# First-layer expert weights in 512 x 512 pieces, and highest scheduler priority for the activations' short instructions

## The chip, the cores and the metric

The kernel runs on one core of one Trainium2 chip. The metric is the device time of one execution in microseconds (us), the median of several runs. The core's engines work side by side, each through its own queue in order: TensorE (PE, matrix products), VectorE (DVE), ScalarE (ACT), GpSimd (POOL) and SyncE (SP, which here issues most transfers). Transfers run on 16 DMA engines. PE writes its sums into PSUM, from which DVE and ACT read.

## The reference

One layer of a small model over 1024 tokens of width 1024: a layer norm, an attention and a recurrence side by side, a projection, and then a mixture of 32 experts, four of them for each token. Only the experts matter here. All of it is float32.

```python
def clamped_swiglu(hh):
    x_glu = jnp.minimum(hh[..., ::2], SWIGLU_LIMIT)
    x_lin = jnp.clip(hh[..., 1::2], -SWIGLU_LIMIT, SWIGLU_LIMIT)
    return x_glu * jax.nn.sigmoid(SWIGLU_ALPHA * x_glu) * (x_lin + 1.0)

def expert_block(args):
    idx, e = args
    u = clamped_swiglu(h_pad[idx] @ w1[e] + b1[e])
    return u @ w2[e] + b2[e]
```

An expert's first matrix w1 is 1024 x 2048 (gate and linear columns alternate), its second, w2, 1024 x 1024. Each token's four results are weighted by the router's gates and added.

## The kernel before

**Stages.** The mixers and the router take the first 985 us or so; the 32 experts follow in one unrolled loop (`moe`), up to about 2400 us, and a last layer norm ends the kernel. Experts are ranked by how many tokens they have. The 21 lower ranks get up to 128 token slots ("thin", `first`); the 11 upper ones get 136 to 192 ("wide", `first_wide`). They run in a mixed order: thin, wide, thin, wide, then nine times thin, thin, wide, and a last thin one.

**Products in split form.** A float32 factor is split into a high part and a rest (`split`, lines 204 to 206): ACT casts to the high part (hi), DVE subtracts it from the source (lo). A product is then hi x hi, hi x lo and lo x hi (`mm`, lines 193 to 195).

**Pieces.** The weights come in pieces of 1 MB, 128 partitions by 2048 (`piece`, line 1378): eight for w1, four for w2. SP issues a piece's transfer into one of five tiles `w`; ACT casts it in two halves (tile `wsh`, line 205) and DVE subtracts in two halves (tile `wsl`, line 206), into one of four pairs of split buffers. A split buffer is free again when PE has used the piece for the last time; ACT's cast of a later piece waits for that.

**Thin experts.** The gathered rows are transposed by PE and split (`flip`: transposes at line 1374, then a cast on ACT and a subtraction on DVE), giving `xTh` and `xTl`. For each quarter q of the 2048 columns, PE adds the bias (line 1472) and then the products into one accumulator of 512 columns. Here a piece of w1 has all 1024 rows of 256 columns, so an accumulator takes two pieces, each for one half of its columns, with products of 256 columns: 48 for a quarter. The activation follows in four short instructions: a sigmoid on ACT (1482), a clamp (1484), a product (1485) and a second product into `u` (1486) on DVE. `flip` transposes and splits `u` into `uTh` and `uTl`, one quarter late; the last flip is put off into `second` (`late`). The second layer multiplies `uT` with pieces of w2, in products of 512 columns.

**Wide experts.** The tokens are the moving side: `xw` holds hi and lo side by side, and 128 columns of w1 are loaded as weights. One piece gives two accumulators (gate and linear, g = 0, 1); each takes eight products with hi weights (line 1525, up to 384 columns) and eight with lo weights (line 1527). Then come the activation's short instructions (lines 1529 to 1539).

**What sets the order.** The program is recorded in the order of the source; a scheduler then places each engine's instructions by simulated readiness and by priority, which goes by the order of the source. Each engine runs its queue in that order.

## Time and profile before

| | |
|---|---|
| median of 3 runs | 2464.48 us (2464.11 to 2464.49) |
| profiled execution, its own time | 2466.53 us |
| its span, first to last instruction | 2464.7 us |
| PE busy | 2286.7 us (93%) |
| DVE busy | 1996.8 us (81%) |
| ACT busy | 1409.1 us (57%) |
| moved | 567.80 MB, mean 230 GB/s |

Busy shares are averages over the span. A matmul's start is recorded, its end is modelled, and several are under way at once; so PE's pace is read from the distance between starts, not from the busy share. An instruction of DVE that follows another of its kind starts before the recorded end of the one ahead. A wait is put down to what ended last.

### The profile page before, as it was taken

How to read it: one execution, taken by the hardware profiler on the slowest of the kernel's cores; microseconds unless marked ns; L12 is line 12 of the kernel's file. 1: busy time of each engine (PE TensorE's matmuls, PEld its weight loads, DVE VectorE, ACT ScalarE, POOL GpSimd, SP SyncE). 2: the span in 40 equal slices, each digit the busy share in tenths (PEclk: the TensorE clock that was granted, in tenths of full speed). 3: DMA queues.
4: the chain of work that ended last, by engine and by line, in shares of the span. 5: the costliest groups of instructions: out<-in, count | busy, mean ns of one | idle time of the engine just before them, and what ended most of it. 6: DMA issues, size and time to landing. Idle time of an engine off the chain costs nothing. (4 is left out here: it accounts for less than half of the span.)

```text
span 2464.7 us, 42046 instructions
## 1 busy us (share of the span) xinstructions
PE 2286.7 (93%) x15539; PEld 1940.2 (79%) x15539; DVE 1996.8 (81%) x3878; ACT 1409.1 (57%) x2355; POOL 549.3 (22%) x411
## 2 busy tenths in 40 slices
PE   6999989999998995899999999999999999999992
PEld 3776766676765784888898998989889898888981
DVE  7666447777776776788898989898989898898977
ACT  5333335455545433666676767676667676666764
POOL 1005222222213533121211212111212121111113
PEclk9999989999898995999999999999999999999996
DMA  6378542212123323978898979897979898888973
GB/s 268 119 263 278 187 112 56 59 45 58 34 41 90 115 96 128 342 283 290 297 335 296 338 288 337 281 358 275 363 252 336 297 334 302 292 326 300 333 272 139
DMA packets 167335, 567.80 MB, mean 230 GB/s; under 512 B 64617, under 2 KB 79738, under 8 KB 116821
## 3 DMA queue, kind: packets, MB, share of 16 engines
q1 hardware_dynamic: 155476, 524.63, 58.2%
q0 software_dynamic: 11216, 39.34, 6.5%
q8 instruction: 124, 2.03, 0.3%
q10 hardware_dynamic: 432, 1.09, 0.1%
q14 instruction: 87, 0.70, 0.1%
HBM read 508.22 MB, written 56.79 MB: 229 GB/s over the span
## 5 line engine op out<-in xcount | busy, mean ns | idle before, releaser
L206 DVE TENSOR_TENSOR wsl<-w,wsh 128x1024 fp32r<-128x1024 f32 x786 | 932.9, 1218 | 143.6 <-ACT wsh L205 142.1
L205 ACT CAST wsh<-w 128x1024 fp32r<-128x1024 f32 x786 | 782.8, 1047 | 346.6 <-PE acc L195 91.9
L193 PE MATMUL acc<-wsh,xTh 128*128 128x256 f32 x1344 | 381.9, 285 | 10.0 <-ACT xTh L205 5.1
L1525 PE MATMUL acc<-xw,wsh 128*128 128x368 f32 (+7 forms) x1408 | 381.1, 354 | 8.0 <-DVE t L1530 8.0
L194 PE MATMUL acc<-wsl,xTh 128*128 128x256 f32 x1344 | 382.9, 285 | 0.7 <-DVE wsl L206 0.7
L195 PE MATMUL acc<-wsh,xTl 128*128 128x256 f32 x1344 | 381.7, 285 | 0.3 <-DVE xTl L206 0.3
L1527 PE MATMUL acc<-xw,wsl 128*128 128x184 f32 (+7 forms) x1408 | 337.9, 240 | 0.0
L1525 PEld LDWEIGHTS acc<-xw,wsh 128*128 128x128 f32 x1408 | 268.9, 191 | 10.1 <-issue 5.4
L1527 PEld LDWEIGHTS acc<-xw,wsl 128*128 128x128 f32 x1408 | 273.3, 194 | 0.7
L193 PEld LDWEIGHTS acc<-wsh,xTh 128*128 128x128 f32 x1344 | 258.5, 193 | 13.2 <-ACT xTh L205 7.0
L194 PEld LDWEIGHTS acc<-wsl,xTh 128*128 128x128 f32 x1344 | 259.4, 193 | 4.8 <-DVE wsl L206 1.0
L195 PEld LDWEIGHTS acc<-wsh,xTl 128*128 128x128 f32 x1344 | 259.2, 193 | 1.8 <-DVE xTl L206 0.6
L1459 POOL DMA_INDIRECT y_d<-y,idx x42 | 143.0, 3405 | 420.5 <-DVE y L1451 333.3
L1362 POOL DMA_INDIRECT xg<-h_d,idx x43 | 97.7, 2273 | 615.7 <-issue 272.2
L193 PE MATMUL acc<-wsh,uTh 128*128 128x512 f32 x512 | 203.5, 400 | 19.2 <-ACT uTh L205 19.2
L194 PE MATMUL acc<-wsl,uTh 128*128 128x512 f32 x512 | 202.4, 396 | 0.0
L195 PE MATMUL acc<-wsh,uTl 128*128 128x512 f32 x512 | 193.6, 406 | 1.3 <-DVE uTl L206 1.3
L193 PEld LDWEIGHTS acc<-wsh,uTh 128*128 128x128 f32 x512 | 97.3, 190 | 40.7 <-ACT uTh L205 21.8
L193 PE MATMUL sm<-hTh,wsh 128*128 128x512 f32 x288 | 115.0, 400 | 6.4 <-ACT wsh L205 2.0
L194 PE MATMUL sm<-hTl,wsh 128*128 128x512 f32 x288 | 115.6, 401 | 4.2 <-DVE hTl L347 3.1
L195 PE MATMUL sm<-hTh,wsl 128*128 128x512 f32 x288 | 113.5, 395 | 0.0
L194 PEld LDWEIGHTS acc<-wsl,uTh 128*128 128x128 f32 x512 | 97.8, 191 | 19.3 <-DVE wsl L206 0.2
(584 smaller groups left out, 4323.5 us busy)
## 6 DMA issues: line engine op xcount, KB each, us to landing
w<-in_w_dram SPq DMA_DIRECT2D x384, 1024.0 KB
aw<-in_ada_dram SPq DMA_DIRECT2D x34, 512.0 KB
w<-in_w_in_dram SPq DMA_DIRECT2D x18, 512.0 KB
aw<-in_ada_dram SPq DMA_DIRECT2D x7, 1024.0 KB
rkv_d<-stage SPq DMA_DIRECT2D x12, 512.0 KB
xt<-in_x_dram SPq DMA_DIRECT2D x8, 512.0 KB
xr<-in_x_dram SPq DMA_DIRECT2D x8, 512.0 KB
xr_d<-xr SPq DMA_DIRECT2D x8, 512.0 KB
```

What stands on the lines that cost most here:

```text
L193: mm(out, a.hi, b.hi, start=start, stop=False)
L194: mm(out, a.hi, b.lo, start=False, stop=False)
L195: mm(out, a.lo, b.hi, start=False, stop=stop)
L205: (hi_eng or self.nc.scalar.copy)(dst.hi, src)
L206: (lo_eng or self.nc.vector).tensor_tensor(dst.lo, src, dst.hi.bitcast(F32), ALU.subtract)
L1362: self.nc.gpsimd.indirect_dma_start(out=xg[0:n], out_offset=None, in_=self.h2_d, in_offset=bass.IndirectOffsetOnAxis(ap=idx[0:n, 0:1], axi ...
L1459: nc.gpsimd.indirect_dma_start(out=self.y_d, out_offset=bass.IndirectOffsetOnAxis(ap=idx[0:n, 0:1], axis=0), in_=y[0:n], in_offset=None, c ...
L1525: nc.tensor.matmul(acc[:, 0:2 * cap], w.hi[:, c], xw[:, k].rearrange("p a t -> p (a t)"), start=(k == 0), stop=False)
L1527: nc.tensor.matmul(acc[:, 0:cap], w.lo[:, c], xw[:, k, 0], start=False, stop=(k == KD - 1))
```

## The change

Three edits, all in the experts.

1. The host lays out w1 so that a piece holds 512 rows of 512 columns (four blocks of 128 rows) instead of 1024 rows of 256. Size and number of the pieces stay.
2. A thin expert's quarter still takes two pieces, but each is now one half of the rows for all 512 columns: 24 products of 512 columns instead of 48 of 256. A wide expert takes two pieces at a time, for two column blocks j; each of its four accumulators needs both.
3. The short instructions of the activations, and the flips of `u`, are recorded under the scheduler's highest priority.

```diff
-    w1 = f("exp_w1")[0].reshape(NE, KD, P, 8, P, 2)
-    o["w1"] = w1.transpose(0, 3, 2, 1, 5, 4).reshape(NE, 8, P, KD, 256)
+    w1 = f("exp_w1")[0].reshape(NE, 2, 4, P, 4, 2, P, 2)
+    o["w1"] = w1.transpose(0, 4, 1, 3, 2, 5, 7, 6).reshape(NE, 8, P, 4, 512)
...
-            for j in range(2):
-                ws = self.piece(w1[bass.ds(e, 1), 2 * q + j].rearrange("o p k n -> (o p) (k n)"))
-                for k in range(KD):
-                    w, c = ws[k // 4], k % 4 * 256
-                    self.mm(acc[:, j * 256:(j + 1) * 256], xT[:, k], w[:, c:c + 256],
-                            start=False, stop=(j == 1 and k == KD - 1))
...
+            for m in range(2):
+                ws = self.piece(w1[bass.ds(e, 1), 2 * q + m].rearrange("o p k n -> (o p) (k n)"))
+                for k in range(4):
+                    c = k % 2 * 512
+                    self.mm(acc, xT[:, 4 * m + k], ws[k // 2][:, c:c + 512], start=False, stop=(m == 1 and k == 3))
+            with self.tc.high_priority():
...
+                S.activation(v2(sg), a[:, :, 0], AF.Sigmoid, scale=1.702)
...
+                if q:
+                    self.flip(uT, u, 2 * q - 2, 2 * q)
+
+        def late():
+            with self.tc.high_priority():
+                self.flip(uT, u, 6, 8)
+        return [uT], late
...
-            ws = self.piece(w1[bass.ds(e, 1), j].rearrange("o p k n -> (o p) (k n)"))
+            if j % 2 == 0:
+
+                ws = []
+                for m in range(2):
+                    ws += self.piece(w1[bass.ds(e, 1), j + m].rearrange("o p k n -> (o p) (k n)"))
...
+                a = j % 2 * 2 + g
                 for k in range(KD):
-                    w = ws[k // 4]
-                    c = slice(k % 4 * 256 + g * P, k % 4 * 256 + (g + 1) * P)
+                    w, c = ws[k // 2], slice(k % 2 * 512 + a * P, k % 2 * 512 + (a + 1) * P)
...
+                with self.tc.high_priority():
+                    t = mp.tile([P, cap], F32, name=f"t{g}")
...
```

In the rows of the built programs below, a name's number tells one buffer's use from another; `wsh_` and `wsl_` with neighbouring numbers are one piece. PE in a thin expert, where one piece of a quarter ends and its other one begins. Before:

```order
L193 MATMUL acc_16542<-wsh_16546,xTh_16300 128x256
L194 MATMUL acc_16542<-wsl_16547,xTh_16300 128x256
L195 MATMUL acc_16542<-wsh_16546,xTl_16301 128x256
L193 MATMUL acc_16542<-wsh_16578,xTh_16300 128x256
L194 MATMUL acc_16542<-wsl_16579,xTh_16300 128x256
L195 MATMUL acc_16542<-wsh_16578,xTl_16301 128x256
```

and now:

```order
L193 MATMUL acc_15606<-wsh_15610,xTh_15436 128x512
L194 MATMUL acc_15606<-wsl_15611,xTh_15436 128x512
L195 MATMUL acc_15606<-wsh_15610,xTl_15437 128x512
L193 MATMUL acc_15606<-wsh_15630,xTh_15436 128x512
L194 MATMUL acc_15606<-wsl_15631,xTh_15436 128x512
L195 MATMUL acc_15606<-wsh_15630,xTl_15437 128x512
```

The products are twice as wide and half as many: twelve of them use up a piece, where 24 did.

PE in a wide expert, from the last products of the second accumulator's first four row blocks on. Before:

```order
L1525 MATMUL acc_15872<-xw_15697,wsh_15846 128x336
L1527 MATMUL acc_15872<-xw_15697,wsl_15847 128x168
L1525 MATMUL acc_15852<-xw_15697,wsh_15846 128x336
L1527 MATMUL acc_15852<-xw_15697,wsl_15847 128x168
L1525 MATMUL acc_15852<-xw_15697,wsh_15846 128x336
```

and now (line 1533 is the former 1525, line 1535 the former 1527):

```order
L1533 MATMUL acc_15016<-xw_14833,wsh_14982 128x336
L1535 MATMUL acc_15016<-xw_14833,wsl_14983 128x168
L1533 MATMUL acc_14996<-xw_14833,wsh_14990 128x336
L1535 MATMUL acc_14996<-xw_14833,wsl_14991 128x168
L1533 MATMUL acc_14996<-xw_14833,wsh_14990 128x336
```

The third row is the 17th product of the expert. It stood on the first piece (wsh_15846), and stands now on the second (wsh_14990); before, the second piece came after all 32 products of the first and twelve of the second layer of the expert ahead.

DVE at the start of the same wide expert, from the first accumulators' read on; `wsl` rows are the weights' subtractions, the third and fourth piece here. Before:

```order
L206 TENSOR_TENSOR wsl_15961<-w_15958,wsh_15960 128x1024 x2
L206 TENSOR_TENSOR uTl_15393<-tr_15767,uTh_15392 128x256
L1339 SCALAR_TENSOR_TENSOR idx_15737<-tr_15728,at_15739 128x1
L1354 TENSOR_REDUCE gate_15738<-tr_15728 128x1
L1530 TENSOR_TENSOR t0_15869<-acc_15852,t0_15869 128x168
L206 TENSOR_TENSOR wsl_16018<-w_16015,wsh_16017 128x1024 x2
L1530 TENSOR_TENSOR t1_15889<-acc_15872,t1_15889 128x168
L1451 SCALAR_TENSOR_TENSOR y_15832<-acc_15745,gate_14797,g2p_8911 128x512
L1451 SCALAR_TENSOR_TENSOR y_15832<-acc_15746,gate_14797,g2p_8911 128x512
L1535 TENSOR_SCALAR t1_15889<-t1_15889 128x168
```

and now (lines 1539, 1545, 1546 and 1547 are the former 1530, 1535, 1536 and 1537):

```order
L1354 TENSOR_REDUCE gate_14874<-tr_14864 128x1
L1539 TENSOR_TENSOR t0_15013<-acc_14996,t0_15013 128x168
L1539 TENSOR_TENSOR t1_15033<-acc_15016,t1_15033 128x168
L1545 TENSOR_SCALAR t1_15033<-t1_15033 128x168
L1546 SCALAR_TENSOR_TENSOR t1_15033<-t0_15013,t1_15033 128x168
L1547 SCALAR_TENSOR_TENSOR t1_15033<-sg_15036,t1_15033 128x168
L1451 SCALAR_TENSOR_TENSOR y_14968<-acc_14881,gate_14125,g2p_8911 128x512
L1451 SCALAR_TENSOR_TENSOR y_14968<-acc_14882,gate_14125,g2p_8911 128x512
L206 TENSOR_TENSOR uTl_14979<-t1_15033,uTh_14978 128x128
L206 TENSOR_TENSOR u1_8914<-t1_15033,u1_8914 128x40
L206 TENSOR_TENSOR wsl_15105<-w_15102,wsh_15104 128x1024 x2
```

The whole chain of the first column block, nine short instructions, now stands ahead of the fourth piece's subtraction, where one stood before.

## Rows read from the trace of the kernel before

**Rows 1.** The page, busy time: us, share of the span, instructions.
```profile
PE 2286.7 (93%) x15539; PEld 1940.2 (79%) x15539; DVE 1996.8 (81%) x3878; ACT 1409.1 (57%) x2355; POOL 549.3 (22%) x411
```
**Rows 2.** Table by stage: stretch, length, busy us by engine, granted clock, DMA share, GB/s.
```profile
core 0: us, PE busy (x) PEld busy (x) DVE busy (x) ACT busy (x) POOL busy (x), PEclk, DMA share, GB/s
1443.00:1480.00 37.00, 37.00 (x259) 34.06 (x258) 35.47 (x43) 27.21 (x34) 8.80 (x2) 1.00 0.87 322
1480.00:1518.00 38.00, 36.91 (x270) 34.07 (x269) 37.33 (x50) 26.61 (x34) 14.24 (x4) 1.00 0.91 333
1518.00:1575.00 57.00, 57.00 (x385) 52.24 (x384) 48.85 (x104) 37.04 (x74) 5.04 (x4) 1.00 0.82 297
1575.00:1611.00 36.00, 36.00 (x256) 33.28 (x255) 35.51 (x44) 27.05 (x33) 7.52 (x2) 1.00 0.91 323
1611.00:1649.00 38.00, 36.90 (x269) 33.93 (x268) 37.34 (x50) 26.59 (x35) 9.70 (x4) 1.00 0.93 343
```
**Rows 3.** PE in time order, a thin first layer: start us, us, engine, line, operation.
```profile
1596.08 0.28 PE L195 MATMUL acc<-wsh,xTl 128*128 128x256 f32 x1
...
1598.96 0.28 PE L195 MATMUL acc<-wsh,xTl 128*128 128x256 f32 x1
```
**Rows 4.** PE in time order, two second layers of thin experts.
```profile
1179.10 0.39 PE L193 MATMUL acc<-wsh,uTh 128*128 128x512 f32 x1
...
1182.05 0.39 PE L194 MATMUL acc<-wsl,uTh 128*128 128x512 f32 x1
...
1607.61 0.40 PE L193 MATMUL acc<-wsh,uTh 128*128 128x512 f32 x1
...
1608.77 0.39 PE L195 MATMUL acc<-wsh,uTl 128*128 128x512 f32 x1
```
**Rows 5.** The page, costliest groups: count | busy us, mean ns | idle before, releaser.
```profile
L193 PE MATMUL acc<-wsh,xTh 128*128 128x256 f32 x1344 | 381.9, 285 | 10.0 <-ACT xTh L205 5.1
L194 PE MATMUL acc<-wsl,xTh 128*128 128x256 f32 x1344 | 382.9, 285 | 0.7 <-DVE wsl L206 0.7
L195 PE MATMUL acc<-wsh,xTl 128*128 128x256 f32 x1344 | 381.7, 285 | 0.3 <-DVE xTl L206 0.3
```
**Rows 6.** PE in time order, start of the wide expert at 1525.
```profile
1525.31 0.41 PE L1525 MATMUL acc<-xw,wsh 128*128 128x336 f32 x1
...
1527.41 0.35 PE L1525 MATMUL acc<-xw,wsh 128*128 128x336 f32 x1
...
1529.26 0.35 PE L1525 MATMUL acc<-xw,wsh 128*128 128x336 f32 x1
...
1532.55 0.31 PE L1525 MATMUL acc<-xw,wsh 128*128 128x336 f32 x1
```
**Rows 7.** DVE in time order, the same expert's second and fourth piece.
```profile
1523.36 2.35 DVE L206 TENSOR_TENSOR wsl<-w,wsh 128x1024 fp32r<-128x1024 f32 x2
...
1530.99 2.36 DVE L206 TENSOR_TENSOR wsl<-w,wsh 128x1024 fp32r<-128x1024 f32 x2 [0.69 <-ACT wsh L205]
```
**Rows 8.** Waits from 985 to 2405 us: us in total, times, longest.
```profile
ACT sg L1482 <- PE acc L195: 62.6, 51, 8.0
ACT wsh L205 <- DMA w<-in_w_dram: 16.0, 10, 4.5
PE acc L193 <- ACT uTh L205: 11.5, 9, 3.0
```
**Rows 9.** PE in time order near 1778 us, and that stretch by stage.
```profile
1778.35 0.50 PE L193 MATMUL acc<-wsh,uTh 128*128 128x512 f32 x1 [2.18 <-ACT uTh L205]
...
1778.94 0.63 PE L193 MATMUL acc<-wsh,uTh 128*128 128x512 f32 x1
1779.36 0.63 PE L194 MATMUL acc<-wsl,uTh 128*128 128x512 f32 x1
...
1775.00:1782.00 7.00, 4.82 (x21) 3.69 (x19) 6.36 (x11) 3.74 (x7) 0.00 (x0) 0.78 1.00 422
```

More of the change, by code (lines that the diff above doesn't have):

```diff
@@ L1472, in first @@
             nc.tensor.matmul(acc, self.pick[:, q:q + 1].to_broadcast([P, P]), bs, start=True, stop=False)
-            for j in range(2):
-                ws = self.piece(w1[bass.ds(e, 1), 2 * q + j].rearrange("o p k n -> (o p) (k n)"))
-                for k in range(KD):
-                    w, c = ws[k // 4], k % 4 * 256
-                    self.mm(acc[:, j * 256:(j + 1) * 256], xT[:, k], w[:, c:c + 256],
-                            start=False, stop=(j == 1 and k == KD - 1))
-            a = acc.rearrange("p (j g f) -> p j g f", j=2, g=2)
-            v2 = lambda t: t.rearrange("p (j f) -> p j f", j=2)
-            sg = mp.tile([P, 256], F32, name="sg")
-            S.activation(v2(sg), a[:, :, 0], AF.Sigmoid, scale=1.702)
-            ln = mp.tile([P, 256], F32, name="ln")
-            V.tensor_scalar(v2(ln), a[:, :, 1], 8.0, -6.0, ALU.min, ALU.max)
-            V.scalar_tensor_tensor(v2(ln), a[:, :, 0], 7.0, v2(ln), ALU.min, ALU.mult)
-            V.scalar_tensor_tensor(u[:, q * 256:(q + 1) * 256], sg, SIG7, ln, ALU.min, ALU.mult)
-            if q:
-                self.flip(uT, u, 2 * q - 2, 2 * q)
-        return [uT], lambda: self.flip(uT, u, 6, 8)
+            for m in range(2):
[4 more added lines that the diff above has]
+            with self.tc.high_priority():
+                a = acc.rearrange("p (j g f) -> p j g f", j=2, g=2)
+                v2 = lambda t: t.rearrange("p (j f) -> p j f", j=2)
+                sg = mp.tile([P, 256], F32, name="sg")
+                S.activation(v2(sg), a[:, :, 0], AF.Sigmoid, scale=1.702)
+                ln = mp.tile([P, 256], F32, name="ln")
+                V.tensor_scalar(v2(ln), a[:, :, 1], 8.0, -6.0, ALU.min, ALU.max)
+                V.scalar_tensor_tensor(v2(ln), a[:, :, 0], 7.0, v2(ln), ALU.min, ALU.mult)
+                V.scalar_tensor_tensor(u[:, q * 256:(q + 1) * 256], sg, SIG7, ln, ALU.min, ALU.mult)
+                if q:
[4 more added lines that the diff above has]
+        return [uT], late
     def load_x(self, rows):
@@ L1527, in first_wide @@
                     nc.tensor.matmul(acc[:, 0:cap], w.lo[:, c], xw[:, k, 0], start=False, stop=(k == KD - 1))
-                t = mp.tile([P, cap], F32, name=f"t{g}")
-                S.activation(t, acc[:, cap:2 * cap], AF.Identity, bias=bc[:, 2 * j + g:2 * j + g + 1])
-                V.tensor_tensor(t, acc[:, 0:cap], t, ALU.add)
-                parts.append(t)
-            gl, ln = parts
-            sg = mp.tile([P, 256], F32, name="sg")[:, 0:cap]
-            S.activation(sg, gl, AF.Sigmoid, scale=1.702)
-            V.tensor_scalar(ln, ln, 8.0, -6.0, ALU.min, ALU.max)
-            V.scalar_tensor_tensor(ln, gl, 7.0, ln, ALU.min, ALU.mult)
-            V.scalar_tensor_tensor(ln, sg, SIG7, ln, ALU.min, ALU.mult)
-            self.split(u0[:, j], ln[:, 0:P])
-            self.split(Split(u1[:, j, 0, 0:n1], u1[:, j, 1, 0:n1]), ln[:, P:cap])
+                with self.tc.high_priority():
+                    t = mp.tile([P, cap], F32, name=f"t{g}")
+                    S.activation(t, acc[:, cap:2 * cap], AF.Identity, bias=bc[:, 2 * j + g:2 * j + g + 1])
+                    V.tensor_tensor(t, acc[:, 0:cap], t, ALU.add)
+                    parts.append(t)
+            with self.tc.high_priority():
+                gl, ln = parts
+                sg = mp.tile([P, 256], F32, name="sg")[:, 0:cap]
+                S.activation(sg, gl, AF.Sigmoid, scale=1.702)
+                V.tensor_scalar(ln, ln, 8.0, -6.0, ALU.min, ALU.max)
+                V.scalar_tensor_tensor(ln, gl, 7.0, ln, ALU.min, ALU.mult)
+                V.scalar_tensor_tensor(ln, sg, SIG7, ln, ALU.min, ALU.mult)
+                self.split(u0[:, j], ln[:, 0:P])
+                self.split(Split(u1[:, j, 0, 0:n1], u1[:, j, 1, 0:n1]), ln[:, P:cap])
         return [u0, u1], None
```

## The prediction

> **What bounds the kernel now.** I read the page's busy list first [rows 1]: TensorE (PE) is busy 93% of the span, VectorE (DVE) 81%, ScalarE (ACT) 57%. That is an average over a mixer part and an expert part, so the table by stage comes next [rows 2]. It covers thin, thin, wide, thin, thin expert from 1443 to 1649 us. In every row PE is busy for at least 36.9 of 38 us at a granted clock of 1.00. DVE is busy for 35.5 of 37, 37.3 of 38 and 37.3 of 38 us in the thin rows, but only for 48.9 of 57 in the wide one. The 16 DMA engines are at 0.82 to 0.93. So PE sets the pace of the experts, DVE follows within 1 to 2 us of every thin expert, and only a wide expert gives DVE time to catch up. The reader should keep these two together: whatever PE saves in two thin experts in a row, DVE has to save as well, or draw from its lead.
>
> A busy PE is not a PE at its peak, so I counted how far apart its products start. The 256-column products of a thin first layer stand 24 steps apart in 1598.96 - 1596.08 = 2.88 us: 0.120 us each [rows 3]. The 512-column products of the second layer make 13 steps in 1182.05 - 1179.10 = 2.95 us, 0.227 us each, and in a slower place 5 steps in 1608.77 - 1607.61 = 1.16 us, 0.232 us each [rows 4]. The second layer's weights come in the same type and through the same split, so these rows stand for the new 512-column products.
>
> **Wider products in thin experts.** 21 thin experts hold 1344 products in each of three lines [rows 5], 4032 in all. They become 2016 of twice the width. Before: 4032 x 0.120 = 483.8 us. After: 2016 x 0.2275 = 458.6 us. That is 25.2 us less on PE; by the slower step, 2016 x 0.232 = 467.7, it is 16.1. I take 25.2, since the clean stretches are the common case, and keep 16 as an end. Nothing covers this work now, so it comes off the path as long as PE stays the bound. Bytes, transfers, casts and subtractions keep their number and size: a piece is 128 x 2048 before and after. Transfers cost nothing by my sum: ACT waited for a weight transfer 10 times, 16.0 us in all [rows 8]; if the cover were gone, one piece would cost at most the longest of those, 4.5 us.
>
> A rule of the Trainium skill speaks against this term. The page TensorE: Matmul & The Clock Gate, section Back-to-back issue gap, gives a warm product's step as its columns over 2.4 GHz plus 2.5 ns: 109.2 ns for 256 columns, 215.8 ns for 512. By that rule halving the count saves 2.5 ns a pair, 5.0 us in all, instead of 25.2. The rows differ from it at both widths (120 and 227 ns), and they decide.
>
> **Pairs of pieces in wide experts.** The same matrix is now cut so that a wide expert needs two pieces before it can end any accumulator. The products of a wide expert keep number, width and weight loads: PE's own time is unchanged. What moves is when the second piece is needed. Before, the first product on the second piece starts at 1532.55, 7.24 us after the first product of the expert at 1525.31 [rows 6]. By the order of the changed program it is the 17th product, behind eight pairs. A pair takes (1529.26 - 1527.41) / 7 = 0.264 us [rows 6], so it is needed after 2.1 us: 5.1 us sooner. Its subtraction on DVE ended at 1523.36 + 2.35 = 1525.71 [rows 7], 6.8 us ahead of need. That cover shrinks to 1.7.
>
> Two more things eat it. First, over the two thin experts ahead PE gains 2 x (192 x 0.120 - 96 x 0.2275) = 2.4 us, while DVE's work there, 35.5 + 37.3 = 72.9 of 74 us [rows 2], stays. Its idle 1.1 us absorb part at best, so 1.3 to 2.4 us of lead are lost. Secondly, the wide expert ahead of the pair now gives its split buffers back later: in the order, five fewer 512-column products lie between the release and the first product of the next thin expert, 5 x 0.2275 = 1.1 us of lead, of which some or none may bite. So the cover ends between 1.7 - 1.3 = +0.4 and 1.7 - 2.4 - 1.1 = -1.8. I take a wait of 1.0 us. There are nine places where two thin experts stand ahead of a wide one: 9 us given back, between 0 and 16.
>
> Inside a wide expert the bursts cost nothing by my sum. The order puts nine short DVE instructions, where one stood, ahead of the fourth subtraction. But DVE is idle there for 57 - 48.9 = 8 us [rows 2], and the fourth piece is first needed behind a whole pair of pieces' products. If that cover were gone, each pair would wait about the 0.7 us that DVE waited for ACT in the row shown [rows 7].
>
> **Highest priority for the short instructions.** It changes places in four queues, not work. On ACT a sigmoid that waits for its accumulator holds the casts queued behind it; PE accumulators kept it waiting 51 times for 62.6 us already, and nobody on PE felt that, since ACT is 57% busy. On PE the transposes of the activations (line 1374) and the second layer's first product stand behind the short chain; PE lost 11.5 us in nine waits for the cast of a transposed activation [rows 8]. By the order the last flip of a thin expert stands some 1.5 us nearer to its accumulator, because PE has less to do between, and the chain on DVE has about as many subtractions in it as before. So I expect these waits neither gone (-11.5) nor doubled (+11.5), but a little more: +0.4 us in each of nine pairs, +4 us. POOL and SP keep their order; POOL's waits are on no path here.
>
> **The clock.** One PE wait of 2.18 us for such a cast was followed by products 0.42 us apart, and that stretch of 7 us was granted 0.78 of the clock [rows 9]: part of it ran at 1.2 instead of 2.4 GHz, and PE lost (1 - 0.78) x 7 = 1.5 us. A wait of 1.0 us is well under 2.18; I take 0, and keep 1.5 us for each of nine places as an end.
>
> **The sum.** -25.2 + 9 + 4 = -12.2 us. The profiled execution took 2466.5 us, 1.8 more than its span of 2464.7 and 2.0 more than the median of the runs, 2464.48. The edit lies wholly in the span, so I take the same difference off the median: 2452 us.
>
> **The rivals.**
> - The cover holds, and no wait comes at the wide experts: then the flips balance too, and PE's 25.2 us all arrive: 2439. For it: DVE's lead in a wide expert is 8 us of idle time. Against it: the cover sums to zero only at its best end.
> - DVE becomes the bound of the thin pairs. If the wait is 2.4 us in each of nine places (22 us) with the flips' 4 us, the gain is gone: 2465. For it: DVE's 72.9 of 74 us. Against it: it needs more than the worse end of my cover.
> - Slower: the wait for the second piece reaches the length after which half speed followed. With 3.0 us of wait and 1.5 us of half speed in nine places and the flips' 4 us the price is 44.5 us against 25.2: 2484. It decides from (25.2 - 4) / 9 = 2.4 us for wait and clock together, which the worst cover, 1.8, passes once half speed follows. For it: [rows 9]. Against: 3.0 us are 1.2 more than the worst cover.
> - The wide product is no bargain: if a first-layer product of 512 columns steps at 0.2375 us, just above the slow rows, PE saves only 5.0 us, and with 13 us given back the time is 2472. Against it: [rows 3, 4]. The rule of the Trainium skill named above (TensorE: Matmul & The Clock Gate, Back-to-back issue gap) gives the same saving by other steps.
>
> **How the numbers follow.** Forecast 0.58, cover holds 0.13, DVE the bound 0.14, half speed 0.10, no bargain 0.05. A measurement of this kernel can tell about 0.2%, 5 us, from no change: 2459.5 to 2469.4. The forecast itself spreads from 2444 to 2460, its give-back running from some 5 to 20 us; a small part of it lies within 0.2%. So faster 0.68 (0.55 + 0.13), same 0.17 (0.03 + 0.14), slower 0.15 (0.10 + 0.05). The range runs from 2438, just under the full saving, to 2468, just over the case where DVE binds; it leaves out half speed and the case of no bargain.
>
> **What would show it.** First-layer products of 512 columns starting 0.227 us apart, 96 to a thin expert plus four bias products, say the first term. PE's busy time and the stretch of a thin pair shrinking by less than 2.4 us, with DVE at 73 of some 73 us, say that DVE binds there. A PE wait of about 1 us for DVE's second subtraction at the start of a wide expert, with its first product on the second piece some 2 us after the first, says the second term. PE waiting for the cast of a transposed activation for clearly more or less than 11.5 us judges the third. The granted clock in those starts judges the slow rival. I am wrong in the main if the steps are not 0.227, or if PE waits inside the wide experts, at each pair of pieces, rather than at their start.

## The result, and the profile after

The changed kernel is **slower**, by 0.57%: 2476.52 us (median; 2463.43 for the kernel before, run beside it). The ratio is 1.0057, with a 95% interval of 1.0043 to 1.0070, so about 14 us are lost where the prediction had 12 gained; the time lies above its range. One of its 22 executions took 3185.47 us at a mean granted clock of 0.643, and is not in the ratio. The profiled execution took 2468.29 us, 8 us under its kernel's median, against 2466.53 before, 3 over. Executions of one kernel differ by some 10 us either way, so sums from two profiles hold to about that, and only ratios over many executions decide below which kernel is faster.

First the page of the changed kernel, busy time, and the three lines that answer to [rows 1, 5] (count | busy us, mean ns | idle before):

```profile
PE 2264.4 (92%) x13523; PEld 1824.5 (74%) x13523; DVE 1997.7 (81%) x3878; ACT 1405.3 (57%) x2353; POOL 482.5 (20%) x411
...
L193 PE MATMUL acc<-wsh,xTh 128*128 128x512 f32 x672 | 263.5, 395 | 4.5 <-ACT wsh L205 4.0
L194 PE MATMUL acc<-wsl,xTh 128*128 128x512 f32 x672 | 264.7, 394 | 0.5 <-DVE wsl L206 0.5
L195 PE MATMUL acc<-wsh,xTl 128*128 128x512 f32 x672 | 264.4, 394 | 0.0
```

The products are half as many. Their steps, PE in time order in a thin first layer (start us, us), nine steps between the two rows:

```profile
1596.42 0.39 PE L195 MATMUL acc<-wsh,xTl 128*128 128x512 f32 x1
...
1598.46 0.39 PE L195 MATMUL acc<-wsh,xTl 128*128 128x512 f32 x1
```

(1598.46 - 1596.42) / 9 = 0.227 us, as [rows 4] had it. So PE saved what was forecast. The table by stage, with the columns of [rows 2], for thin, thin, wide, thin, thin of the changed kernel, shows where it went:

```profile
1439.60:1478.70 39.10, 36.16 (x148) 28.07 (x147) 35.89 (x44) 26.53 (x33) 7.31 (x2) 0.92 0.89 339
1478.70:1519.40 40.70, 38.37 (x194) 31.15 (x193) 38.19 (x51) 28.36 (x37) 5.11 (x4) 0.99 0.84 300
1519.40:1575.90 56.50, 56.50 (x377) 51.76 (x377) 47.60 (x100) 35.76 (x71) 3.65 (x3) 1.00 0.79 283
1575.90:1615.10 39.20, 36.11 (x148) 28.17 (x147) 35.93 (x45) 26.63 (x33) 6.55 (x2) 0.92 0.89 336
1615.10:1655.90 40.80, 38.46 (x195) 31.13 (x193) 38.20 (x52) 28.34 (x37) 5.43 (x4) 0.99 0.84 299
```

A thin pair (two thin experts in a row) took 74 us before [rows 2] and takes 39.2 + 40.8 = 80.0 now. The wide expert shown is nearly unchanged. Over the loop it looks otherwise: counted from an expert's first product on PE (the bias product, in a thin one) to the next expert's first one, the nine thin pairs took 680.2 us before and take 702.5 now, and the eleven wide experts took 634.3 and take 620.5. So the pairs lose 22 us and the wide experts win 14; both come back below. In both thin rows PE *and* DVE stand idle for some 2.3 to 3.3 us: neither is the bound any more. What PE waited for, from 985 to 2405 us (us in total, times, longest):

```profile
PE acc L193 <- ACT uTh L205: 20.5, 17, 1.9
PE acc L195 <- DVE uTl L206: 13.5, 11, 1.7
PE tr L1330 <- DVE uTl L206: 10.6, 9, 1.2
...
PE tr L1374 <- DVE uTl L206: 3.7, 10, 0.4
PE acc L1533 <- DVE t L1539: 3.2, 1, 3.2
PE tr L1374 <- DVE u L1486: 1.3, 1, 1.3
```

All but the line of L1533 are waits on the flips of `u` (three of them through the buffers of the transposes and through `u` itself): 49.6 us. Before, the same view had 11.5 us for uTh [rows 8] and these lines:

```profile
PE acc L1525 <- DVE t L1530: 8.0, 8, 2.0
...
PE acc L195 <- DVE uTl L206: 1.3, 2, 1.1
PE tr L1374 <- DVE u L1486: 0.7, 1, 0.7
```

That makes 13.5 us on flips, so there are 36 us of new waits against some 28 us of work saved. The wide experts' wait for DVE's read of an accumulator (L1525, now L1533) fell from 8.0 to 3.2 us.

One place of a flip, at the end of the first layer of the thin expert that starts at 1576 us. PE, DVE and ACT in time order (in brackets, idle time ahead and what ended it):

```profile
1604.59 0.79 PE L1374 MATMUL tr<-csts,u 128*128 128x128 f32 x4
1607.14 0.50 PE L193 MATMUL acc<-wsh,uTh 128*128 128x512 f32 x1 [1.77 <-ACT uTh L205]
...
1610.15 1.22 PE L195 MATMUL acc<-wsh,uTl 128*128 128x512 f32 x2 [0.93 <-DVE uTl L206]
```
```profile
1604.47 0.41 DVE L1486 SCALAR_TENSOR_TENSOR u<-sg,ln 128x256 f32<-128x256 f32 x1
1604.80 3.49 DVE L206 TENSOR_TENSOR wsl<-w,wsh 128x1024 fp32r<-128x1024 f32 x3
1608.21 0.42 DVE L1485 SCALAR_TENSOR_TENSOR ln<-acc,ln 128x256 f32<-128x256 f32 x1
1608.54 1.22 DVE L206 TENSOR_TENSOR wsl<-w,wsh 128x1024 fp32r<-128x1024 f32 x1
1609.67 0.42 DVE L206 TENSOR_TENSOR uTl<-tr,uTh 128x256 fp32r<-128x256 f32 x1
```
```profile
1604.83 1.99 ACT L205 CAST wsh<-w 128x1024 fp32r<-128x1024 f32 x2 [0.71 <-PE acc L195]
1606.73 0.36 ACT L205 CAST uTh<-tr 128x256 fp32r<-128x256 f32 x1
```

The four transposes are done by 1605.4. The cast `uTh` stands behind two casts of weights on ACT, and `uTl` behind four subtractions of weights on DVE. In PE's queue nothing stands between the transposes and the first product on `uTh`, so PE idles twice, 2.7 us in all. The clock follows (table by stage of the two stretches, granted clock third from the end of each row):

```profile
1604.00:1611.00 7.00, 3.91 (x15) 2.37 (x14) 7.00 (x12) 2.92 (x6) 0.00 (x0) 0.86 1.00 404
1611.00:1616.00 5.00, 5.00 (x13) 3.84 (x13) 1.76 (x4) 1.99 (x2) 0.00 (x0) 0.51 0.82 338
```

For 5 us PE was granted 0.51, so it ran nearly all the time at 1.2 instead of 2.4 GHz, which costs (1 - 0.51) x 5 = 2.5 us more. Over all experts, though, the clock is the same in both kernels, by the third number from the end of the two rows (before, then after):

```profile
965.00:2430.00 1465.00, 1406.99 (x9684) 1290.56 (x9684) 1315.09 (x2119) 984.17 (x1509) 272.50 (x103) 0.98 0.84 305
```
```profile
965.00:2430.00 1465.00, 1389.34 (x7651) 1180.67 (x7652) 1309.29 (x2113) 979.47 (x1505) 201.31 (x101) 0.98 0.83 304
```

**A budget of PE.** From the first bias product of the experts to the last product of a second layer I took each step from one start to the next. The median step of its form (line, tiles and shapes) is work; an excess of about one more such step is half speed; an excess above 0.3 us is a wait; what is left is small excess. In us, from one profile each (the other kernels are explained below):

| kernel | length | work | half speed | waits | small |
|---|---|---|---|---|---|
| before | 1460.4 | 1367.4 | 23.1 | 62.2 | 7.7 |
| after | 1468.8 | 1338.9 | 22.9 | 91.1 | 15.9 |
| new pieces, products of 256 | 1463.6 | 1369.4 | 20.8 | 65.4 | 8.0 |
| old pieces, clamp on ACT | 1424.4 | 1366.1 | 14.1 | 37.4 | 6.8 |
| new pieces, clamp on ACT | 1410.6 | 1338.5 | 11.5 | 45.4 | 15.2 |

How finely the forms are told apart moves some 3 us between work, half speed and small excess; the length and the waits stay. Before to after: work -28.5, waits +28.9, small excess +8.2, half speed -0.2.

### The profile page after: what moved, and what is told of

Its sections match the earlier page's. It is cut to its first block, busy times and chain, and to the rows that moved or that the text cites. A ratio compares the mean times of both kernels' runs of the same rounds, so it can differ in the third digit from the quotient of the medians.

```text
span 2466.2 us, 38048 instructions
## 1 busy us (share of the span) xinstructions
PE 2264.4 (92%) x13523; PEld 1824.5 (74%) x13523; DVE 1997.7 (81%) x3878; ACT 1405.3 (57%) x2353; POOL 482.5 (20%) x411
## 3 DMA queue, kind: packets, MB, share of 16 engines
q8 instruction: 108, 1.77, 0.3%
## 4 chain that ended last, share of the span: by engine, by line
PE 33%; DVE 20%; issue 5%; ACT 2%; DMA 1%; SPq 0%; POOLq 0%; POOL 0%; DVEq 0%; ACTq 0%
DVE wsl L206 14%; PE acc L1533 11%; PE acc L195 6%; PE acc L193 5%; PE acc L194 5%; PE acc L1535 4%; ACT wsh L205 1%; DMA w<-in_w_dram 1%; PE tr L1374 1%; PE acc L1439 1%; PE acc L1435 1%; DVE ln L1484 1%; DVE uTl L206 1%; DVE oh L1326 1%; DVE y L1451 1%
## 5 line engine op out<-in xcount | busy, mean ns | idle before, releaser
L1533 PE MATMUL acc<-xw,wsh 128*128 128x368 f32 (+7 forms) x1408 | 373.7, 350 | 3.3 <-DVE t L1539 3.2
L1533 PEld LDWEIGHTS acc<-xw,wsh 128*128 128x128 f32 x1408 | 265.0, 189 | 4.7 <-issue 3.4
L193 PE MATMUL acc<-wsh,xTh 128*128 128x512 f32 x672 | 263.5, 395 | 4.5 <-ACT wsh L205 4.0
L194 PE MATMUL acc<-wsl,xTh 128*128 128x512 f32 x672 | 264.7, 394 | 0.5 <-DVE wsl L206 0.5
L195 PE MATMUL acc<-wsh,xTl 128*128 128x512 f32 x672 | 264.4, 394 | 0.0
L193 PE MATMUL acc<-wsh,uTh 128*128 128x512 f32 x512 | 207.8, 409 | 28.5 <-ACT uTh L205 22.1
L1459 POOL DMA_INDIRECT y_d<-y,idx x42 | 121.6, 2896 | 490.7 <-DVE y L1451 382.2
L195 PE MATMUL acc<-wsh,uTl 128*128 128x512 f32 x512 | 201.4, 418 | 13.6 <-DVE uTl L206 13.5
L1362 POOL DMA_INDIRECT xg<-h_d,idx x43 | 58.9, 1370 | 624.1 <-DVE xTl L206 221.5
L193 PEld LDWEIGHTS acc<-wsh,xTh 128*128 128x128 f32 x672 | 127.7, 190 | 31.3 <-ACT wsh L205 4.2
L194 PEld LDWEIGHTS acc<-wsl,xTh 128*128 128x128 f32 x672 | 127.5, 190 | 28.0 <-DVE wsl L206 1.0
L195 PEld LDWEIGHTS acc<-wsh,xTl 128*128 128x128 f32 x672 | 127.3, 189 | 26.9 <-DVE xTl L206 0.2
L195 PEld LDWEIGHTS acc<-wsh,uTl 128*128 128x128 f32 x512 | 96.8, 197 | 40.3 <-DVE uTl L206 21.6
```

The source lines that it names most:

```text
L193: mm(out, a.hi, b.hi, start=start, stop=False)
L194: mm(out, a.hi, b.lo, start=False, stop=False)
L195: mm(out, a.lo, b.hi, start=False, stop=stop)
L1362: self.nc.gpsimd.indirect_dma_start(out=xg[0:n], out_offset=None, in_=self.h2_d, in_offset=bass.IndirectOffsetOnAxis(ap=idx[0:n, 0:1], axi ...
L1459: nc.gpsimd.indirect_dma_start(out=self.y_d, out_offset=bass.IndirectOffsetOnAxis(ap=idx[0:n, 0:1], axis=0), in_=y[0:n], in_offset=None, c ...
L1533: nc.tensor.matmul(acc[:, 0:2 * cap], w.hi[:, c], xw[:, k].rearrange("p a t -> p (a t)"), start=(k == 0), stop=False)
```

## The experiments

Theories, by the letters that the expectations use. **A**: the raised priority places the flips badly. **B**: the chain from a quarter's accumulator to its flip keeps its length, while PE with wider products reaches the flip's first use sooner. **C**: DVE paces the thin pairs, whatever PE is seen to wait for. **D**: the wide experts' pairs of pieces cost the lead. **E**: the split buffers limit how far ACT and DVE run ahead. **F**: the cut of the pieces itself costs. Each ratio is to the kernel before on the same chip, with its 95% interval.

**The priority.** New pieces without any raised priority (`e1`); old pieces with it (`e2`); new pieces with it in thin (`e3`) or wide experts (`e4`) alone.

```diff
-            with self.tc.high_priority():
+            if True:
```

> The new pieces (512 rows x 512 columns, thin and wide experts) without any raised priority. Theory A (the raised priority places the flips of u badly): the waits of PE on the cast and the subtraction of u's transposes, 48 us in the changed kernel (uTh 20.5, uTl 13.5, transposed slots behind uTl 10.6, transposes behind uTl 3.7) against 13 before, fall back to about 13, and the 25 us saved on PE arrive: 12 to 25 us faster than before, 2440 to 2452. Theory B (the shape alone: PE has less to do between a quarter's end and the first use of its flip, while the casts and subtractions queued ahead of the flip are as many): those waits stay near 48 us and the kernel is within 0.3% of the changed one, 5 to 20 us slower than before. Theory C (DVE paces the thin pairs): the waits go from the flips to the subtractions of weights, and the time stays within 5 us of before.

> The pieces of before (1024 rows x 256 columns) with the raised priority at all the places of the change. Theory A: PE's waits on the flips of u rise from 13 us to 40 us or more, and the kernel is 20 to 40 us slower than before. Theory B: the waits stay within 10 us of before's 13, the time within 0.3% of before. Theory C: as B.

> The new pieces in both kinds of expert, the raised priority only in the thin experts. If A holds through the thin experts' flips, this is as slow as the changed kernel (within 0.2%). If the harm comes from the wide experts' short instructions under raised priority (they run ahead of casts and subtractions of the pieces that the next thin expert needs), it is as fast as the kernel without any priority. Theory B: as the changed kernel within 0.3%.

> The new pieces in both kinds of expert, the raised priority only in the wide experts: the other half of the pair. A through the thin experts' flips: as fast as the kernel without any priority, 12 to 25 us under before. A through the wide experts: as slow as the changed kernel. Theory B: as the changed kernel within 0.3%.

Measured: e1 1.0069 (1.0044 to 1.0093), e2 0.9993 (0.9968 to 1.0018), e3 1.0070 (1.0043 to 1.0097), e4 1.0068 (1.0044 to 1.0092). A falls: the priority is worth nothing, and the pieces are the whole loss. The order of the experts' instructions in the traces says why. With the new pieces, taking the priority away changes the instruction at 2 of 7668 places on PE, 2 of 1511 on ACT and 6 of 2141 on DVE, and each of PE's waits on flips is the same to 0.3 us. So what the front's order rows show of bunched short instructions comes from the pieces, not from the priority.

**Which expert, and which part of the cut.** From here on the new pieces come without raised priority. `e5` has new pieces in thin experts alone, `e6` in wide ones alone (a second copy of the weights in the other layout serves the rest). `e13` has new pieces in both, but two products of 256 columns for one of 512:

```diff
-                    self.mm(acc, xT[:, 4 * m + k], ws[k // 2][:, c:c + 512], start=False, stop=(m == 1 and k == 3))
+                    for h in range(0, 512, 256):
+                        self.mm(acc[:, h:h + 256], xT[:, 4 * m + k], ws[k // 2][:, c + h:c + h + 256],
+                                start=False, stop=(m == 1 and k == 3 and h == 256))
```

> The new pieces in the thin experts alone; a second copy of the weights in the old layout serves the wide experts, whose code is as before; no raised priority. The run with the new pieces and no priority was 0.69% slower than before, so the pieces are the cause; this one tells in which kind of expert. Theory B (in the thin experts PE runs short of work between the end of a quarter and the first use of its flip; DVE and ACT reach the flip no sooner): the full loss is here, 10 to 20 us slower than before. Theory D (the pairs of pieces in the wide experts cost the lead that the thin ones need): the loss is not here, and the 25 us of PE arrive: 12 to 25 us faster than before.

> The new pieces in the wide experts alone; the thin ones have the old layout and the old code, 256 columns to a product; no raised priority. Theory B: within 5 us of before. Theory D: PE gains nothing in the thin experts and the wide ones lose what the whole change lost beside its gain: 20 to 40 us slower than before.

> New pieces in both kinds of expert, no raised priority, but a thin expert's first layer multiplies each 512-column block in two products of 256 columns, as before the change; PE has the 28 us back that the profile shows it lost. Theory B (the products' width: what PE no longer does in products comes back as waits for the flips, and more): within 0.3% of before, 8 to 15 us under the same kernel with 512 columns, with some 30 us fewer waits of PE. Theory F (the cut of the pieces itself costs, whatever the products' width): 15 to 30 us above the kernel with 512 columns, 2490 to 2505.

Measured: e5 1.0125 (1.0096 to 1.0154), e6 1.0018 (0.9995 to 1.0041), e13 1.0019 (0.9999 to 1.0038). The thin experts hold the loss, as B says, and more of it than the whole change (28 us, where B had 10 to 20): the wide experts' pairs of pieces give back about 0.6% where the thin experts have the new pieces, though alone they win nothing. D falls, and so does F: the new cut with the old width is as fast as before, within the interval. It is the **width of the products** that costs, by 0.5%, though it takes work off PE. PE's waits of e13, in the same view as above:

```profile
PE tr L1330 <- DVE uTl L206: 12.7, 9, 1.4
PE acc L193 <- ACT uTh L205: 8.9, 11, 0.9
...
PE acc L195 <- DVE uTl L206: 3.3, 9, 0.5
PE tr L1374 <- DVE uTl L206: 1.1, 2, 0.8
```

26.0 us on flips, where 512 columns give 49.6. But 26.0 is already twice the 13.5 of before. `e6`, whose thin experts are as before, has 27.8 us of these waits, and its instructions stand in the same order as e13's on ACT and DVE and, but for a dozen places, on PE. So some 13 of the 36 us of new waits come with the wide experts' pairs of pieces, and some 23 with the width. The first part costs no time, because the wide experts win as much. Length and PE's waits by kind of expert, counted and told apart as above, in us, from one profile each:

| kernel | nine thin pairs | waits there | eleven wide experts | waits there |
|---|---|---|---|---|
| before | 680.2 | 19.7 | 634.3 | 14.4 |
| e6, new pieces in wide experts alone | 695.1 | 30.5 | 619.0 | 3.7 |
| e13, new pieces, products of 256 | 693.1 | 30.8 | 619.2 | 3.9 |
| after | 702.5 | 56.3 | 620.5 | 3.7 |

The flips show how both parts arise. I read three means from the traces, over the first experts of the nine pairs, for quarters 0, 1 and 2 (us): the chain from the end of a quarter's accumulator to `u`; PE's work, in median steps, between that end and the first product on the quarter's flip; and how long before its first product `uTl` is ready.

| kernel | chain to `u` | PE's work until the first use | `uTl` ready ahead by |
|---|---|---|---|
| before | 8.7, 8.1, 8.1 | 18.2, 15.4, 13.5 | 2.4, 1.8, 2.4 |
| e13 | 11.4, 11.0, 11.2 | 18.2, 15.2, 13.7 | 0.1, 0.1, 0.3 |
| after | 11.9, 10.4, 12.0 | 17.3, 14.2, 13.1 | (PE waits) |

The wide experts' pairs of pieces make the chain there 3 us longer: 8 to 9 subtractions of weights stand in it, where 6 to 7 stood. In e6 the three chains are the same to 0.1 us. That uses up the lead of the flips, and PE just gets by. The wide product then takes 0.6 to 1.0 us of PE's work away over each flip, 2.5 us in a pair and some 22 in nine, and PE's waits in these experts rise from 4.0 us in e13 to 25.5. That is B, on top of a chain that had grown. As a mean over all 72 quarters of the pairs the chain is as long as ever (9.2 us before, 8.7 in e13, 9.0 after), which hides this, because it is shorter in the second experts' first quarter (8.9 before, 4.4 after).

One thing stays open. With the width the scheduler's order changes too: the first flip of such an expert had 5.1 us of PE's work between its transposes and its first use before, 1.9 in e13 and 0.5 with 512 columns. No run holds the order and changes the width alone, so the share of this placing is not known.

**Without the dependence.** In `e7` (new pieces) and `e8` (before) a thin expert's second layer multiplies the split rows of x, while the flips still run.

```diff
-            self.second(e, slots[i], uT, late, i == NE - 1)
+            u2 = [x[i]] if late else uT
+            self.second(e, slots[i], u2, late, i == NE - 1)
```

> New pieces in both kinds of expert, no raised priority; the second layer of a thin expert multiplies the split rows of x in the place of the split activations, so nothing on PE but the transposes themselves depends on a flip of u. The flips are still carried out, and DVE, ACT and PE have the same number of instructions. It leaves out the use of the activations, and its output isn't the reference's. Theory B (latency of the flips): PE's waits for uTh and uTl, 34 us in the kernel with the flips, go, and no others come: 25 to 35 us under that kernel (2474.8 in the runs before), 2440 to 2450. Theory C (DVE paces the thin pairs, whatever PE waits on): PE waits as long for the subtractions of weights or for split buffers, and the time stays within 8 us of the kernel with the flips in use.

> The kernel before with the same cut: thin experts' second layers multiply the split rows of x. Leaves out the use of the activations. It is the floor for the old pieces: PE waited there 13 us for uTh and uTl, so both theories expect 0 to 15 us under before, about 2450. Under B the kernel with the new pieces and the same cut is some 20 us faster than this one (the 25 us of products), under C it is no faster.

Measured: e7 1.0207 (1.0178 to 1.0235), e8 1.0200 (1.0174 to 1.0225). Both are slower, which no theory expected, so this decides nothing. With the dependence gone the scheduler built another order, with waits of its own: e8 waited 33.9 us for gathered rows, e7 40 us for buffers of transposes behind `uTl`.

**Relief of DVE.** The scaling of the result goes to ACT and POOL, in the new pieces (`e9`) and before (`e10`):

```diff
-  nc.vector.scalar_tensor_tensor(yh, a[h][0:n], gate[0:n], self.g2p[0:n, sl], ALU.mult, ALU.mult)
+  nc.scalar.activation(yh, a[h][0:n], AF.Copy, scale=gate[0:n])
+  nc.gpsimd.tensor_tensor(yh, yh, self.g2p[0:n, sl], ALU.mult)
```

> New pieces, no raised priority; the scaling of the second layer's result (line 1451, two DVE instructions of 0.74 us in a thin expert) goes to ACT (times the gate) and POOL (times the row of the last modulation). DVE loses 1.5 us of some 36 to 38 in each expert, the chain from a quarter's accumulator to its flip is untouched. Theory C (DVE paces the thin pairs): 2 x 1.5 us in each of nine pairs come back, 20 to 30 us under the kernel without the relief, so 2445 to 2455 where that took 2475, and under before. Theory B (latency of the flips): within 8 us of the kernel without the relief.

> The kernel before with the same relief of DVE. PE was busy for all but 1 to 2 us of every thin expert, so under both theories it wins little: 0 to 10 us under before. Under C the new pieces with relief end 5 to 20 us under this one; under B they stay 8 us or more above it.

Measured: e9 1.0061 (1.0037 to 1.0086), e10 0.9957 (0.9936 to 0.9978). By the expectation this speaks against C, but the trace of e9 shows that it was no relief (busy line, subtractions of weights):

```profile
PE 2271.5 (92%) x13523; PEld 1828.9 (74%) x13523; DVE 2009.7 (81%) x3814; ACT 1445.3 (58%) x2419; POOL 724.4 (29%) x475
...
L206 DVE TENSOR_TENSOR wsl<-w,wsh 128x1024 fp32r<-128x1024 f32 x786 | 956.4, 1253 | 128.5 <-ACT wsh L205 128.2
```

64 instructions of 0.74 us, 47 us, left DVE, and its busy time rose, from 1994.2 us in e1 to 2009.7; the subtractions alone went from 927.3 to 956.4. So e9 leaves C where it was. In e10, too, DVE's busy time rose, from 1996.8 to 2000.9 us, so its 0.4% is not a saving of DVE's busy time; where it comes from is not shown.

**More lead.** Four pairs of split buffers of a piece become eight of half a piece, in the new pieces (`e11`) and before (`e12`):

```diff
-        ws = self.split_tile(mp, [P, 2048], "ws", bufs=SBUF)
-        for c in CUT:
-            self.split(ws[:, slice(*c)], w[:, slice(*c)])
+        ws = [self.split_tile(mp, [P, 1024], "ws", bufs=2 * SBUF) for _ in CUT]
+        for t, c in zip(ws, CUT):
+            self.split(t, w[:, slice(*c)])
```

> New pieces, no raised priority; the four pairs of split buffers of a piece become eight pairs of half a piece, same memory, so a cast may begin when PE has used half a piece. Theory E (neither PE nor DVE is the bound: both stand idle in turn, since ACT's casts wait for PE to give split buffers back, DVE waits for the casts, and PE waits for a flip queued behind them on DVE): half a piece, 12 products of 0.227 us x 1/2 = 1.4 us more lead, takes 5 to 20 us off the time without it. Theory C: within 5 us of it, since DVE's work is the same. Theory B: within 5 us.

> The kernel before with half-piece split buffers. PE has little to win there: 0 to 10 us under before by theory E, within 5 us by B and C.

> The kernel before with split buffers of half a piece and the scaling of the result on ACT and POOL, each of which took some 10 us off before. If the two act on different waits they add up: 2436 to 2442 where before takes 2459, 0.7 to 0.9% under it. If both act on the same wait: about 2448, as each alone. A candidate for a kernel faster than both.

Measured: e11 1.0011 (0.9989 to 1.0032), e12 0.9952 (0.9934 to 0.9970). The lead is worth 0.5 to 0.6% with either pieces, as E says, so it does not explain the difference between them. Halves and e10's edit together on the old pieces (`e14`) gave 1.0044 (1.0019 to 1.0069): two gains of 0.4 to 0.5% that turn into a loss when joined, where 0.7 to 0.9% or one of the two gains was expected.

**A shorter chain.** In `e16` (new pieces) and `e17` (before) a plain copy on ACT, behind the sigmoid, takes the place of DVE's clamp of the linear part, so these two leave out the clamp.

```diff
-  V.tensor_scalar(v2(ln), a[:, :, 1], 8.0, -6.0, ALU.min, ALU.max)
+  S.copy(v2(ln), a[:, :, 1])
```

`e18` (new pieces) and `e20` (before) keep the clamp, in two steps on ACT (`lim` holds 8 and 14), and DVE does two steps for three (lines of the diff that only set up `lim` are left out):

```diff
-  V.tensor_scalar(v2(ln), a[:, :, 1], 8.0, -6.0, ALU.min, ALU.max)
-  V.scalar_tensor_tensor(v2(ln), a[:, :, 0], 7.0, v2(ln), ALU.min, ALU.mult)
-  V.scalar_tensor_tensor(u[:, q * 256:(q + 1) * 256], sg, SIG7, ln, ALU.min, ALU.mult)
+  S.activation(v2(ln), a[:, :, 1], AF.Relu, bias=self.lim[:, 0:1], scale=-1.0)
+  S.activation(ln, ln, AF.Relu, bias=self.lim[:, 1:2], scale=-1.0)
+  V.scalar_tensor_tensor(v2(sg), a[:, :, 0], 7.0, v2(sg), ALU.min, ALU.mult)
+  V.scalar_tensor_tensor(u[:, q * 256:(q + 1) * 256], ln, 6.0, sg, ALU.subtract, ALU.mult)
```

> New pieces, no raised priority; the clamp of the linear part on DVE (line 1484) is replaced by a plain copy on ACT, right behind the sigmoid. It leaves out the clamp at 8 and -6. The chain from a quarter's accumulator to its flip has one step less on DVE, and so two subtractions (2.3 us) less to stand behind; DVE loses 4 x 0.34 = 1.4 us in a thin expert, about as much as in the run that relieved it elsewhere and won nothing. Theory B (latency of the chain): the waits of PE on flips, 50 us, fall by a third or more, 15 to 35 us under the kernel with the clamp (2475). Theory C: as the run with relief, within 5 us of 2475.

> The kernel before with the same cut (clamp left out, copy on ACT). PE waited 13 us on flips there. Theory B: 5 to 15 us under before, so less than the new pieces win by it. Theory C: 5 to 10 us under before, as with the relief of DVE.

> New pieces, no raised priority; nothing is left out. In thin experts ACT forms the clamped linear part in two steps of its own, r = relu(8 - l), then relu(14 - r), and DVE does two steps where it did three: the gate's clamp times the sigmoid, then (the second relu - 6) times that; the minimum on the sigmoid, which differs from the sigmoid by under 0.00001, goes. Theory B (latency of the chain through DVE's queue): one step less to stand behind subtractions; ACT's second step stands right behind its first or behind one or two casts of 1.05 us. 2430 to 2445 where before takes 2460, so 0.6 to 1.2% under before and 30 to 45 us under the new pieces alone. Theory C: within 5 us of the new pieces alone, 2475.

> The kernel before with the same clamp on ACT. Theory B: 2435 to 2450, so 0.4 to 1.0% under before, and 5 to 15 us above the new pieces with the same clamp, since with the short chain the wide products' saving of 28 us of work is no longer all eaten.

Measured: e16 0.9872 (0.9842 to 0.9903), e17 0.9903 (0.9873 to 0.9933), e18 0.9878 (0.9854 to 0.9902), e20 0.9857 (0.9834 to 0.9880). The chain from accumulator to `u`, as the mean of the 72 quarters, fell from 9.0 us to 6.2 in e16 and 6.1 in e18, and from 9.2 to 5.6 in e17 and 5.4 in e20. The new pieces win 2.0 and 1.9% by it against e1, 47 to 48 us; DVE's busy time fell by 24 to 26 us (1994.2 in e1, 1968.1 and 1970.2 here), so even if each of those counted, nearly half of the gain is left to the latency. That speaks for B, though the edit mixes the two and their shares stay open. PE's waits of e18:

```profile
PE acc L195 <- DVE uTl L206: 7.9, 2, 7.6
...
PE tr L1374 <- DVE uTl L206: 2.3, 7, 0.4
PE tr L1374 <- DVE u L1487: 1.3, 1, 1.3
PE acc L193 <- ACT uTh L205: 0.7, 2, 0.4
```

12.2 us are left of 49.6, and 7.6 of them are one wait outside the nine pairs; e20 has 8.7. But the old pieces win 1.0 and 1.4% too, 24 and 35 us, more than the 5 to 15 and 10 to 25 us that B gave them. And the pairs e16 to e17 and e18 to e20 differ by -0.3% and +0.2%, less than their intervals, where B had the old pieces with the short chain 5 to 15 us behind the new ones. The loss of the wide products is gone; their gain is still not seen. The tables by stage say why, thin, thin in e18, then in e20:

```profile
1567.30:1601.70 34.40, 34.40 (x159) 27.68 (x157) 34.40 (x40) 30.22 (x42) 15.84 (x2) 1.00 0.90 331
1601.70:1640.80 39.10, 38.19 (x189) 30.81 (x189) 38.57 (x53) 31.16 (x46) 12.04 (x4) 1.00 0.94 348
```
```profile
1573.30:1609.40 36.10, 36.10 (x253) 33.37 (x252) 34.73 (x40) 29.83 (x41) 5.17 (x2) 1.00 0.90 323
1609.40:1646.70 37.30, 36.84 (x274) 34.25 (x273) 36.76 (x49) 29.73 (x43) 10.47 (x4) 1.00 0.93 345
```

Both pairs of thin experts take 73.5 and 73.4 us. In e18 DVE is busy for 73.0 of its 73.5. PE is recorded busy for 72.6, but a busy PE is not at its peak: over the nine pairs its work, in median steps, is 622.9 of 652.7 us, while DVE is idle for 10.4. So with the waits gone **DVE is the bound** there, as C says, and most of PE's saving has nowhere to go: the nine pairs take 652.7 us in e18 and 657.9 in e20, 5 us less for 23 us less work. This is read from one profile each; no run takes work off DVE and leaves the chain as it is. In the wide experts e18's profile is 8 us shorter, but it is the shortest of its executions (2421.36 of 2421.36 to 2439.23) beside one that is the longest of e20's (2433.50); the medians, 2431.83 and 2427.74, don't show it, so that stays open. e20, the old pieces with the clamp on ACT, and e18 are faster than both kernels of this case.

## Why the prediction was wrong

- **Wider products in thin experts: right in size, wrong in what it is worth.** The step was forecast at 0.2275 us and is 0.227; the work that went is 28.5 us by the budget, for 25.2. The rule of the Trainium skill that stood against it (TensorE: Matmul & The Clock Gate, section Back-to-back issue gap: 215.8 ns a product, 5.0 us saved) is given there for a product by itself; of a stream of weight loads and products, which this is, the section says that both set the step, about 131 ns for 512 columns. The rows, at 227 ns, differ from both, and the measurement decides. But "it comes off the path as long as PE stays the bound" did not hold. [rows 2] had a first answer: DVE busy for 72.9 of 74 us in a thin pair leaves 1.1 us, and over the nine pairs of the trace before DVE is idle for 16.1 us. More than that can't be won there unless DVE draws on its idle time in the wide experts. The prediction said that whatever PE saves there DVE must save as well, and then charged that limit only as lost cover at the wide expert.
- **Highest priority: the step that failed is the price of the flips under this heading.** The priority itself is worth 0, not +4. The flips were to cost a little more, "neither gone (-11.5) nor doubled (+11.5)", +0.4 us in each pair. Measured: PE's waits on flips went from 13.5 to 49.6 us, +36, none of it from the priority, some 23 from the width of the products and some 13 from the wide experts' pairs of pieces. Two premises failed. "About as many subtractions in it as before" holds for the last flip, but the first three chains of a pair's first expert have two more each. And the prediction did write that PE has less to do between, but looked at the last flip of an expert alone, where PE's work from accumulator to first use even grew (from 15.1 to 16.5 us in the first experts). The loss of cover lies at the first three flips. The trace before had what it takes to price the width: the chain has its length from the subtractions that it stands behind, 6 to 7 of 1.2 us in 8.1 to 8.7 us, which PE's speed doesn't touch.
- **Pairs of pieces in wide experts: wrong, by 9 us at the place that was priced.** No wait came. At the wide expert after 1525 us the first product on the second piece starts 2.19 us after the expert's first, as forecast (2.1), but its subtraction (DVE, 1523.76 + 2.36 = 1526.12) is 1.3 us ahead of it:

```profile
1525.24 0.40 PE L1533 MATMUL acc<-xw,wsh 128*128 128x336 f32 x1
...
1527.43 0.35 PE L1533 MATMUL acc<-xw,wsh 128*128 128x336 f32 x1
```
```profile
1523.76 2.36 DVE L206 TENSOR_TENSOR wsl<-w,wsh 128x1024 fp32r<-128x1024 f32 x2
```

  In the nine such places the margin is 1.2 to 1.4 us. The term took lead off DVE because PE would run ahead of it. Lead was lost, but at the flips: e6's thin pairs take 15 us more than before. And the sum has no gain in the wide experts, where e6 wins 15 us, nearly 11 of them waits. The two cancel: alone the pairs of pieces cost 0.18%, within their interval of nothing.
- **Clock and transfers at 0: right in sum, the clock by luck.** The clock is 0.98 in both kernels over the experts, with 23.1 and 22.9 us of half speed. But places like [rows 9] came in the thin pairs, where half speed rose from 6.4 to 12.5 us, and went elsewhere; in the place shown, waits of 1.77 and 0.93 us went before, shorter than the 2.18 us that the prediction went by. ACT's waits for weight transfers fell from 16.0 us [rows 8] to 3.7.
- **The rivals.** "DVE becomes the bound of the thin pairs" (2465, chance 0.14) is the nearest in mechanism. e18 shows it as the limit once the flips are out of the way, but in the changed kernel DVE is idle for 2.5 to 3.3 us of each thin expert shown, so the flips bind before it. "No bargain" is the nearest in time (2472), but its step of 0.2375 us didn't come. "Half speed" expected a wait for the second piece, which did not come either. No rival had the flips as the mechanism, and that is why the range was too narrow: its upper end, just over the case where DVE binds, still had the flips at +4.

## What to carry to other kernels

When one engine is made faster in a loop that others nearly fill, look first at the second engine's idle time in that very stage: unless that engine can draw on idle time elsewhere, it is the most that can be won. Then count, in the program's order, how much work the faster engine still has between each chain's start and its first use, at every link and not only at the last, and in each expert by itself: a mean over all of them hid the change here. A chain whose length comes from standing in other engines' queues doesn't shrink with it. Shorten such a chain by a step before speeding up what covers it: here one step fewer on DVE was worth 1.0 to 1.4% to the old kernel, and the wider products nothing beside it.

## What the runs showed that was not expected

- POOL's multiplications slow DVE. With 64 of them (128 x 512, median 2.27 us, longest 16.5) in e9, the 112 subtractions on DVE that overlap with one take 1.46 us on the mean and the other 674 take 1.22; the longest one among the experts takes 2.32 us, where it took 1.24 in the changed kernel. What the two contend for no run here shows. The Trainium skill has a rule that fits (SBUF — State Buffer, section SBUF: two separate sides): a GpSimd instruction that reads SBUF and a DVE instruction with two inputs in SBUF share a pair of ports, and the one that comes second is blocked until the other is done. The subtractions have two such inputs, `w` and `wsh`, and the multiplications read `y` and `g2p`.
- Raised scheduler priority moved 10 of some 11,300 instructions of three engines in the new kernel's experts. With the old pieces it moved more (332 of 9684 places on PE differ), and the time did not change either (e2).
- Two edits that win 0.43% and 0.48% alone lose 0.44% together. Each edit makes the scheduler build another order; PE's waits on flips in the joined kernel are 28.9 us, where they were 13.5 before.
